# Making 31 halved products whole, moving cross attention's sums and one last addition, and one more warm product

## The chip, the cores and the metric

The kernel runs on one NeuronCore of one Trainium2 chip. The metric is the device time of one execution in microseconds (us). Kernels are compared by the median of several executions.

## The reference

Two decoder layers work on 256 positions of width 1024, all in float32. Each layer adds a mixer, a cross attention into a memory of 256 rows, and a gated MLP to the residual stream; a last RMSNorm follows.

```
for layer in range(2):
    hn = rmsnorm(h, norm_mix_g[layer])
    h = h + (sb_moba_mixer(hn, ...) if layer == 0 else fox_mixer(hn, ...))      # 16 heads of 64, q/k/v and output projections
    h = h + memory_cross_attention(rmsnorm(h, norm_xa_g[layer]),                # 4 heads of 64, 256 keys
                                   rmsnorm(mem, norm_mem_g[layer]), w_q, w_kv, w_out)
    h = h + conv_ffn(rmsnorm(h, norm_ffn_g[layer]), ...)                        # 1024 -> 2 x 2816 -> conv, silu, gate -> 1024
return rmsnorm(h, final_norm_g)

def rmsnorm(x, g):
    return x * rsqrt(mean(x * x) + 1e-6) * g
```

Layer 0 mixes with eight stick-breaking heads and eight heads with rotary softmax attention, layer 1 with sixteen forgetting heads.

## The kernel before

The residual stream lies transposed in SBUF: eight tiles `h[k]` of 128 channels by 256 positions. Every dense product is made in three pieces: weight and activation are each split into a high part (`whi`, `xh`, written by ScalarE) and a low part (`wlo`, `xl`, written by VectorE), and high times high, high times low and low times high are added up in PSUM. A projection to 128 output channels, `proj` (line 306), is therefore 24 products of 128x128 by 128x256: eight channel tiles, three pieces each, counted by `n`. Its transposed twin `proj_nat` (line 335) makes 128 positions by 256 channels, for the values, with 24 products as well. The weights come as blocks of 128x1024 by DMA (`block`, line 127), seven raw buffers and five split ones ahead.

Each product goes through `product` (line 298). For the places `n` that are listed in `halve` it issues two matmuls of 128 columns with the same weights instead of one of 256:

```
def product(ps, st, mv, halves, **kw):
    if halves:
        kw["skip_group_check"] = True
        for c in (slice(0, P), slice(P, T)):
            nc.tensor.matmul(ps[:, c], st, mv[:, c], **kw)
    else:
        nc.tensor.matmul(ps, st, mv, **kw)
```

Which products are halved is written by hand: for the mixers in the table `HALVES` (line 37; a dictionary for each layer, from a projection's name, such as `q3`, `k0`, `v2`, `o7` or `mk`, to its places), elsewhere as an argument. In the profile whole products have line 304 and halved ones line 302.

TensorE's order is the order of the code (a manual schedule); the other engines' order is made by a scheduler from the same code. A projection can be interrupted at a place `n` by a hook, which issues attention work or norm work there.

A norm's factor is made in three steps. `sums` (line 273) adds the squares over channels by small matmuls with ones; VectorE scales them (`ms`, line 281); GpSimd raises them to the power -1/2 (`rcol`, line 285). `spread` (line 289) turns that column into a row by two transposes on TensorE. The norm's gain is applied to the activations before the product, and the factor only when the product's result is read, so the products don't wait for it.

Cross attention (`cross`, line 827) makes two q projections over the first seven channel tiles, then the eighth for both; `sums` is a hook at 9 in the second. VectorE copies the results to `mq`. Then come the value projections of the memory, whose first has a hook at 8: `scores` makes the score products of four heads (line 799), which VectorE reduces to maxima (line 807), ScalarE exponentiates and VectorE normalises (`xp`, line 816). After the second value projection TensorE transposes the four heads' weights (line 822). The MLP (`ffn`, line 886) has `sums` as a hook at 6 of its second pair's first block, and `spread` at 11 of that pair's second block.

At the end `finish_last` (line 1037) makes the last norm: ScalarE sums the squares of a last part, GpSimd adds them to the rest (line 1050) and raises the mean to the power (line 1051), ScalarE and VectorE scale the rows, and two DMAs write them out. At the start `warm_up` (line 231) issues `WARM` matmuls of zeros, 128x512 in bfloat16, while the first data arrive.

Of the kernel before, what the change touches and what calls it, by code (L numbers as in the profile page):

```python
# [14 lines left out]
ALU = mybir.AluOpType  # L15
# [3 lines left out]
T = 256  # L19
# [3 lines left out]
DFF = 2816  # L23
KF = DFF // P
BLK = 1024
WARM = 9
RAW = 4
LATER = -200

# [4 lines left out]
          ((6, (), (0, 1), ()), (9, (), (), (0, 1)), (11, (0, 1), (2, 3), ()), (14, (), (), (2, 3)),  # L34
           (16, (2, 3), (4, 5), ()), (19, (), (), (4, 5)), (21, (4, 5), (6, 7), ()), (24, (), (), (6, 7)),
           (26, (6, 7), (), ())))
HALVES = ({"v1": (3,), "q3": (8,), "v2": (3, 27), "v3": (25, 29), "o3": (8,), "o7": (2,)},
          {"q0": (21,), "k0": (18, 21), "q1": (8,), "v1": (2,), "q3": (3,), "k3": (8,), "v2": (3,), "q6": (8,), "mk": (8,), "o2": (8,),
           "o7": (2,)})
EPS = 1e-6  # L40
SCALE = DH ** -0.5
MASKED = -1e30
# [38 lines left out]
def trunk(ctx: ExitStack, tc: tile.TileContext, a: dict, out: bass.AP):  # L81
    nc = tc.nc
# [23 lines left out]
    def bank(pl, tag, width=512):  # L106
        return pl.tile([P, 512], F32, tag=tag, name=tag)[:, :width]

    def accA():
        return bank(psA, "acc", T)  # L110

    def accS():
        return bank(psS, "sc", T)
# [491 lines left out]
    mem = Stats("m")  # L605
# [4 lines left out]
    def mixer(layer, st, xs):  # L610
# [47 lines left out]
        for g in range(4):  # L658
# [27 lines left out]
            if g == 0 and layer == 0:  # L686

                accs = [accS() for _ in range(4)]
                for n, (xh, xl) in enumerate(xs):
                    b, o = b0[n // 2], (n % 2) * 4 * P  # L690
                    steps = [(b.hi, xh), (b.hi, xl), (b.lo, xh)]
                    for group in ((0, 1), (2, 3)) if n < 2 else (range(4),):
                        for m, (wt, x) in enumerate(steps):
                            for i in group:
                                product(accs[i], wt[:, o + i * P:o + (i + 1) * P], x, n == 1 and m == 2 and i == 3,
                                        start=n == 0 and m == 0, stop=n == KD - 1 and m == 2)
                b = [block(w[i]) for i in (2, 3, 6)]
                nc.sync.dma_start(const[:, :T], a["const"][:, :T])
                st.rows(a["xt"])
                b.append(block(w[7]))  # L700
                st.sums()
                pv = [proj_nat(b, xs, t, accA()) for t in range(2)]
                early = proj(b[2], 0, xs, accA(), hooks={9: lambda: st.spread(bank(psO, "po"))}, halve=(11,))
                late_constants()
                v = [evac_col(ps, st, t, "v", 6) for t, ps in enumerate(pv)]
                for i in range(2):
                    q, k = (evac_row(accs[2 * i + j], st, "qk"[j], j == 0) for j in range(2))
                    launch(i, q, k, v)
                steps = rope_angles()
                next(steps)  # L710
                for i in range(12):
                    pipe.at(1 + i // 3, lambda: next(steps, None))
                continue
            elif g == 0:
                f = bank(psO, "po", T)

                def rates():
                    gates(f)
                    st.sums()

                q, more = pair(0, ({20: rates}, {15: st.spread}))
                k = more()
                q, k = evac_row(q, st, "q", True), evac_row(k, st, "k", False)
                decay = decay_rows(f, st)
            else:
                q, k = pair(0)
# [100 lines left out]
    def cross(layer, st, xs, ms, ks):  # L827

        hd = []
        bq = [block(a["xa_q"][layer, i]) for i in range(2)]  # L830
        acc = [proj(bq[i], 0, xs[:7], accS(), last=False, hooks={9: st.sums} if i else {}, halve=(11, 14) if i else (2,))
               for i in range(2)]
        for i in range(2):
            proj(bq[i], 7 * P, xs[7:], acc[i], first=False)
        for i in range(2):
            q = parts.tile([P, T], F32, tag="part", name="mq", bufs=NP)
            evac = nc.vector.tensor_scalar(q, acc[i], SCALE, None, op0=ALU.mult)
            hd += [Cross(j, q, ks[i], st) for j in range(2)]
        fence(2, None, evac)

        def scores():
            both_products(hd[:2])
            both_products(hd[2:])
            found = [x.scores() for x in hd]
            fence(1, None, found[-1])

        b = [block(a["xa_v"][layer, i]) for i in range(2)]
        v = [evac_col(proj_nat(b, ms, 0, bank(psO, "po", T), hooks={8: scores}, halve=(14, 17)), mem, 0, "mv", 2)]
        v.append(evac_col(proj_nat(b, ms, 1, accA(), halve=(2, 5)), mem, 1, "mv", 2))
        copied = [x.weigh(nc.vector.tensor_copy if i % 2 else nc.scalar.copy) for i, x in enumerate(hd)]  # L850
        fence(2, *copied[2:])

        def outp(pr):
            po = accA() if pr else bank(psO, "po", T)
            for m in range(2):
                for i in range(2):
                    c = slice((2 * pr + i) * DH, (2 * pr + i + 1) * DH)
                    nc.tensor.matmul(po[i * DH:(i + 1) * DH], v[m][:, c], hd[2 * pr + i].pt[:, m * T:(m + 1) * T],
                                     start=m == 0, stop=m == 1)
            r = act_pair("g", NG)  # L860
            split_ps(po, *r)
            return r

        outs = [outp(0), outp(1)]
        nst, nxt = Stats(one=True), Normed(h, G_FFN + 8 * layer, "x", NX, 2)
        b = [block(a["xa_o"][layer, i]) for i in range(2)]


        def part(j, ps, k, steps=(0, 1, 2), halve=None):
            s = slice(((j % 4) * 2 + k) * P, ((j % 4) * 2 + k + 1) * P)  # L870
            w, (xh, xl) = b[j // 4], outs[k]
            for n in steps:
                product(ps, (w.hi, w.lo, w.hi)[n][:, s], (xh, xh, xl)[n], n == halve, start=k == 0 and n == 0,
                        stop=k == 1 and n == 2)
            return ps

        acc = [part(j, (accA, accA, accS, accS)[j](), 0, (0, 1)) for j in range(4)]
        for j in range(4):
            part(j, acc[j], 0, (2,))
        for j in range(KD):  # L880
            if j >= 4:
                acc.append(part(j, (accA, accA, accS, accS)[j % 4](), 0))
            residual(j, part(j, acc[j], 1, halve=1 if j == 0 else None), nst, nxt)
        return nst, nxt.res

    def ffn(layer, st, xs):
# [58 lines left out]
        for f in range(KF):  # L945
            u = tmp.tile([P, 2 * T], F32, tag="wide", name="u", bufs=5) if f < RAW else None
            c = tmp.tile([P, 2 * T], F32, tag="wide", name="c", bufs=5)
            pss = []
            for i in range(2):
                if f == 0:  # L950
                    pss.append(first[i])
                    continue
                hooks = ({6: st.sums}, {11: st.spread})[i] if f == 1 else {}
                w = block(a["up"][layer, 2 * f + i], pieces=2 if f == 1 and i == 0 else 1)

                pair = layer == 1 and KF - 6 <= f < KF - 2
                if pair:
                    if i == 0:
                        full.append(bank(*((psO, "po"), (psA, "acc"), (psS, "sc"), (psS, "sc"))[f - KF + 6]))
                    acc = full[-1][:, i * T:(i + 1) * T]  # L960
                else:
                    acc = (accS, accA)[i if full else n % 7 % 2]()
                    n += 1
                pss.append(proj(w, 0, xs if f < RAW else xn, acc, first=not (pair and i), hooks=hooks,
                                skip=pair, halve=((8, 11), (13, 20))[i] if f == 1 else ()))
            if f == 0:
                held = u, c, pss
                continue
            if f == KF - 2:
                spare = pss[1]  # L970
            for args in ([(0,) + held] if f == 1 else []) + [(f, u, c, pss)]:
                with tc.high_priority(offset=LATER if f < 6 else 0):
                    glu(*args)
            if f == 1:
                renorm()
            if layer == 1 and 8 <= f < 8 + KD:
                turn_blocks(f - 8)
            if layer == 1 and f == 11 + KD:
                move_blocks()
# [13 lines left out]
    def down_rows(gs, acc, spare):  # L993
# [43 lines left out]
        def finish_last(multiply):  # L1037
# [3 lines left out]
            for i, (ps, c, e) in enumerate(parts[1]):  # L1041
# [5 lines left out]
                if i == 1:  # L1047
                    nc.vector.scalar_tensor_tensor(ms, both[:, 1:2], 1.0 / D, ms, op0=ALU.mult, op1=ALU.add)
                    nc.vector.tensor_mul(o[1][:, :T], ps, gain[1][:, :T])
            nc.gpsimd.tensor_tensor(mean, both[:, 2:3], ms, op=ALU.add)  # L1050
            nc.gpsimd.tensor_tensor(col, mean, half[:, 0:1], op=ALU.pow)
            nc.scalar.activation(o[0], o[0], AF.Copy, scale=col)
            nc.scalar.dma_start(out[P:T, 0:512], o[0])
# [115 lines left out]
```

## Time and profile before

| | |
|---|---|
| time, median of 3 runs | 654.72 us (653.89 to 655.59) |
| the profiled execution's own time | 655.62 us |
| its span, first to last instruction | 653.8 us |
| mean granted TensorE clock | 0.999 |
| TensorE busy, matmuls and weight loads | 646.0 and 632.5 us |
| VectorE, ScalarE, GpSimd busy | 532.6, 433.1 and 72.8 us |
| read from HBM | 119.90 MB |

In the rows below, PE is TensorE's matmuls, PEld its weight loads, DVE VectorE, ACT ScalarE, POOL GpSimd. A row of the timeline has the start in us from the span's start, the time in us, the engine, the line, the operation, the tiles (written <- read), the shape and the number of merged instructions, and in brackets the engine's idle time ahead of it with what ended it. Rows with xN are N instructions that follow each other, from the first's start to the last's end. A row of the stretches has the stretch, its length, and for each engine its busy time and the instructions in it. A row of the waits has the engine and what it waited for: us in total, times, longest.

### The profile page before, as it was taken

To read this page: it belongs to the slowest core of one execution; us is meant where nothing else is said; L and a number is where in the kernel's file an instruction comes from. 1 tells how busy PE (TensorE), PEld (TensorE's weight loads), DVE (VectorE), ACT (ScalarE), POOL (GpSimd) and SP (SyncE) were. 2 spreads that over 40 slices of the span, in tenths; PEclk is the share of its full clock that TensorE was granted. 3 is DMA by queue.
4 is the path that set the end of the run, shared out by engine and by line. 5 is a ranking of instruction groups with operands and counts; after the bars stand their busy time and mean duration, and the time that the engine had idled before them with its cause. 6 is when DMAs were issued, how large, how long until landed. Compare 5 with 4: busy or idle time off the path is not lost.

```text
span 653.8 us, 14673 instructions
## 1 busy us (share of the span) xinstructions
PE 646.0 (99%) x5665; PEld 632.5 (97%) x5665; DVE 532.6 (81%) x1105; ACT 433.1 (66%) x871; POOL 72.8 (11%) x85
## 2 busy tenths in 40 slices
PE   8999999999999999999999999999999999999996
PEld 7999999999999999999999999999999999999996
DVE  6779985999999999865679877868999999996442
ACT  6699764778777776644464676556878767784332
POOL 0001000406100000011114220022350000000000
PEclk9999999999999999999999999999999999999999
DMA  8976651555466666666648654425365667696601
GB/s 317 377 254 217 200 190 48 181 165 189 154 190 212 206 220 184 181 200 198 211 153 309 205 177 148 134 76 190 101 236 182 195 210 214 171 339 193 194 3 64
DMA packets 47669, 124.02 MB, mean 190 GB/s; under 512 B 13648, under 2 KB 17520, under 8 KB 47600
## 3 DMA queue, kind: packets, MB, share of 16 engines
q1 hardware_dynamic: 47168, 122.53, 57.8%
q8 instruction: 44, 0.72, 0.5%
q10 hardware_dynamic: 432, 0.56, 0.3%
q14 instruction: 25, 0.20, 0.1%
HBM read 119.90 MB, written 1.07 MB: 185 GB/s over the span
## 4 chain that ended last, share of the span: by engine, by line
PE 98%; DMA 1%; ACT 0%; POOLq 0%; issue 0%; DVE 0%; ACTq 0%; DVEq 0%; POOL 0%
PE acc L304 49%; PE sc L304 29%; PE acc L1010 3%; PE sc L1010 3%; PE po L1010 2%; PE po L451 2%; PE po L304 2%; PE sc L416 1%; PE sc L436 1%; PE acc L302 1%; DMA raw<-ab_first 1%; PE sc L799 1%; PE sc L822 1%; PE sc L400 0%; PE sc L379 0%; PE acc L278 0%
## 5 line engine op out<-in xcount | busy, mean ns | idle before, releaser
L136 DVE TENSOR_TENSOR wlo<-raw,whi 128x512 fp32r<-128x512 f32 (+2 forms) x288 | 269.8, 958 | 54.4 <-ACT whi L135 52.9
L135 ACT ACTIVATE whi<-raw 128x512 fp32r<-128x512 f32 (+2 forms) x288 | 225.5, 815 | 91.9 <-PE acc L304 37.9
L304 PE MATMUL sc<-xn,whi 128*128 128x256 f32 x656 | 112.9, 276 | 0.0
L304 PEld LDWEIGHTS sc<-xn,whi 128*128 128x128 f32 x656 | 98.9, 188 | 0.0
L304 PE MATMUL sc<-xn,wlo 128*128 128x256 f32 x328 | 90.5, 276 | 0.0
L304 PE MATMUL acc<-xn,whi 128*128 128x256 f32 x464 | 80.3, 276 | 0.0
L304 PE MATMUL acc<-xh,whi 128*128 128x256 f32 x284 | 79.8, 281 | 0.0
L304 PE MATMUL acc<-xl,whi 128*128 128x256 f32 x286 | 79.3, 277 | 0.0
L304 PE MATMUL acc<-xh,wlo 128*128 128x256 f32 x281 | 78.1, 278 | 0.0
L304 PEld LDWEIGHTS acc<-xn,whi 128*128 128x128 f32 x464 | 70.0, 188 | 0.0
L304 PE MATMUL acc<-gh,whi 128*128 128x256 f32 x240 | 67.1, 280 | 0.0
L304 PE MATMUL acc<-gl,whi 128*128 128x256 f32 x240 | 66.3, 278 | 0.0
L253 POOL TENSOR_TENSOR sq<-sq 128x256 f32<-128x256 f32 x35 | 31.4, 896 | 304.5 <-ACT sq L247 288.7
L304 PE MATMUL acc<-gh,wlo 128*128 128x256 f32 x234 | 64.6, 277 | 0.0
L304 PE MATMUL acc<-xn,wlo 128*128 128x256 f32 x232 | 64.0, 276 | 0.0
L304 PEld LDWEIGHTS sc<-xn,wlo 128*128 128x128 f32 x328 | 61.6, 188 | 0.0
L304 PEld LDWEIGHTS acc<-xl,whi 128*128 128x128 f32 x286 | 53.8, 188 | 0.0
L304 PEld LDWEIGHTS acc<-xh,whi 128*128 128x128 f32 x284 | 53.4, 188 | 0.4
L304 PEld LDWEIGHTS acc<-xh,wlo 128*128 128x128 f32 x281 | 52.8, 188 | 0.0
L304 PEld LDWEIGHTS acc<-gh,whi 128*128 128x128 f32 x240 | 45.1, 188 | 1.1 <-ACT gh L183 0.8
L304 PEld LDWEIGHTS acc<-gl,whi 128*128 128x128 f32 x240 | 44.9, 188 | 0.0
L304 PEld LDWEIGHTS acc<-gh,wlo 128*128 128x128 f32 x234 | 43.9, 188 | 0.0
(291 smaller groups left out, 1544.6 us busy)
## 6 DMA issues: line engine op xcount, KB each, us to landing
raw<-up SPq DMA_DIRECT2D x88, 512.0 KB, 4.0
raw<-fox_in SPq DMA_DIRECT2D x24, 512.0 KB, 4.3
raw<-down_rows SPq DMA_DIRECT2D x22, 512.0 KB, 4.4
raw<-ab_in SPq DMA_DIRECT2D x20, 512.0 KB, 6.6
raw<-down SPq DMA_DIRECT2D x16, 448.0 KB, 3.4
raw<-ab_out SPq DMA_DIRECT2D x8, 512.0 KB, 4.6
raw<-down SPq DMA_DIRECT2D x8, 512.0 KB, 3.5
raw<-fox_out SPq DMA_DIRECT2D x8, 512.0 KB, 4.1
```

The lines of the kernel that those rows point to most:

```text
L135: i = nc.scalar.activation(hi[:, s], raw[:, s], AF.Copy)
L136: j = nc.vector.tensor_sub(lo[:, s], raw[:, s], hi[:, s].bitcast(F32))
L253: nc.gpsimd.tensor_tensor(sq, sq, self.acc, op=ALU.add)
L302: nc.tensor.matmul(ps[:, c], st, mv[:, c], **kw)
L304: nc.tensor.matmul(ps, st, mv, **kw)
L416: nc.tensor.matmul(s[:, c], q[:, qs], k[:, 0:n], start=i == 0, stop=True, skip_group_check=True)
L436: nc.tensor.transpose(self.s[:, c:c + P], self.p[:, c:c + P], ident)
L451: nc.tensor.matmul(po[i * DH:(i + 1) * DH, j * T + q:(j + 1) * T], v[m][:, vc + i * DH:vc + (i + 1) * DH], hd.pt[:, c], start=m == 0 and j ...
L799: nc.tensor.matmul(s[:, t * T:(t + 1) * T], self.q[:, t * P:(t + 1) * P], self.k, start=t == 0, stop=True, skip_group_check=True)
L822: nc.tensor.transpose(self.s[:, m * T + t * P:m * T + (t + 1) * P], self.p[:, t * T + m * P:t * T + (m + 1) * P], ident)
L1010: nc.tensor.matmul(ps[:, o:o + T], x[:, s], y[:, c + o:c + o + T], start=False, stop=k == KF - 1 and x is gl, skip_group_check=True)
```

## The change

- 31 of the 46 halved products become whole; 15 stay halved. Five entries go from the table for layer 0 (both places of `v2`, both of `v3`, the one of `o7`) and five from that for layer 1 (`q0`, 21 of `k0`, `q3`, `k3`, `o7`). `early` loses one, each layer's cross attention all seven (three in the q projections, four in the values), and each layer's MLP three of four (20 of the second block stays).
- Cross attention's `sums` moves from place 9 of the second q projection into `scores`, in front of the score products, and that hook moves from place 8 to place 4.
- The addition of `mean` in `finish_last` moves from GpSimd to VectorE.
- `WARM` goes from 9 to 10.

```
-WARM = 9
+WARM = 10
...
-HALVES = ({"v1": (3,), "q3": (8,), "v2": (3, 27), "v3": (25, 29), "o3": (8,), "o7": (2,)},
-          {"q0": (21,), "k0": (18, 21), "q1": (8,), "v1": (2,), "q3": (3,), "k3": (8,), "v2": (3,), "q6": (8,), "mk": (8,), "o2": (8,),
-           "o7": (2,)})
+HALVES = ({"v1": (3,), "q3": (8,), "o3": (8,)},
+          {"k0": (18,), "q1": (8,), "v1": (2,), "v2": (3,), "q6": (8,), "mk": (8,), "o2": (8,)})
...
-                early = proj(b[2], 0, xs, accA(), hooks={9: lambda: st.spread(bank(psO, "po"))}, halve=(11,))
+                early = proj(b[2], 0, xs, accA(), hooks={9: lambda: st.spread(bank(psO, "po"))})
...
-        acc = [proj(bq[i], 0, xs[:7], accS(), last=False, hooks={9: st.sums} if i else {}, halve=(11, 14) if i else (2,))
-               for i in range(2)]
+        acc = [proj(bq[i], 0, xs[:7], accS(), last=False) for i in range(2)]
...
         def scores():
+            st.sums()
             both_products(hd[:2])
...
-        v = [evac_col(proj_nat(b, ms, 0, bank(psO, "po", T), hooks={8: scores}, halve=(14, 17)), mem, 0, "mv", 2)]
-        v.append(evac_col(proj_nat(b, ms, 1, accA(), halve=(2, 5)), mem, 1, "mv", 2))
+        v = [evac_col(proj_nat(b, ms, 0, bank(psO, "po", T), hooks={4: scores}), mem, 0, "mv", 2)]
+        v.append(evac_col(proj_nat(b, ms, 1, accA()), mem, 1, "mv", 2))
...
-                                skip=pair, halve=((8, 11), (13, 20))[i] if f == 1 else ()))
+                                skip=pair, halve=(20,) if f == 1 and i else ()))
...
-            nc.gpsimd.tensor_tensor(mean, both[:, 2:3], ms, op=ALU.add)
+            nc.vector.tensor_add(mean, both[:, 2:3], ms)
```

On TensorE, in layer 0's cross attention, the built order around the sums (`acc<-const,sq`) and the scores (`sc<-mk,mq`) is before:

```order
L304 MATMUL sc<-xh,wlo 128x256
L278 MATMUL acc<-const,sq 128x1 x2
L304 MATMUL sc<-xh,whi 128x256
L304 MATMUL sc<-xl,whi 128x256
L302 MATMUL sc<-xh,wlo 128x128 x2
L304 MATMUL sc<-xh,whi 128x256
L304 MATMUL sc<-xl,whi 128x256
L302 MATMUL sc<-xh,wlo 128x128 x2
```

The sums stood inside the second q projection, with two halved products close behind them. Now the place where the sums stand reads:

```order
L303 MATMUL po<-whi,gh 128x256
L303 MATMUL po<-wlo,gh 128x256
L303 MATMUL po<-whi,gl 128x256
L303 MATMUL po<-whi,gh 128x256
L277 MATMUL acc<-const,sq 128x1 x2
L798 MATMUL sc<-mk,mq 128x256 x8
L303 MATMUL po<-wlo,gh 128x256
```

The sums have moved behind the whole q projection and four value products, right in front of the scores; lines are one lower in the changed file.

On VectorE, at the same place, the order is before (`ms` is the scaled sum, `mq` the copied q, `mx` the maxima):

```order
L188 SCALAR_TENSOR_TENSOR xl<-h_97,small,xh 128x256
L136 TENSOR_TENSOR wlo<-raw,whi 128x512 x4
L281 TENSOR_SCALAR ms<-acc 128x2
L837 TENSOR_SCALAR mq<-sc 128x256 x2
L136 TENSOR_TENSOR wlo<-raw,whi 128x512 x2
L807 TENSOR_REDUCE mx<-sc 128x2 x2
L808 TENSOR_TENSOR mx<-mx,rcol 128x2 x2
```

and now:

```order
L187 SCALAR_TENSOR_TENSOR xl<-h_97,small,xh 128x256
L135 TENSOR_TENSOR wlo<-raw,whi 128x512 x4
L835 TENSOR_SCALAR mq<-sc 128x256 x2
L135 TENSOR_TENSOR wlo<-raw,whi 128x512
L280 TENSOR_SCALAR ms<-acc 128x2
L135 TENSOR_TENSOR wlo<-raw,whi 128x512
L806 TENSOR_REDUCE mx<-sc 128x2 x2
L807 TENSOR_TENSOR mx<-mx,rcol 128x2 x2
```

The scaled sum has moved behind `mq` and one weight split, and has one split between itself and the reduces.

## The prediction

> **What bounds the kernel now.** I read the page first: its busy shares and the chain that ended last.
>
> ```profile
> PE 646.0 (99%) x5665; PEld 632.5 (97%) x5665; DVE 532.6 (81%) x1105; ACT 433.1 (66%) x871; POOL 72.8 (11%) x85
> PE 98%; DMA 1%; ACT 0%; POOLq 0%; issue 0%; DVE 0%; ACTq 0%; DVEq 0%; POOL 0%
> ```
>
> 98% of the chain is TensorE itself. The view of waits, for PE, agrees: it has two entries, both at the program's start.
>
> ```profile
> PE acc L236 <- DVE warm L233: 1.2, 1, 1.2
> PE sc L304 <- ACT whi L223: 0.6, 1, 0.6
> ```
>
> So the question is what one product costs on PE. The view of stretches gives it for a long undisturbed piece of the second MLP, and the timeline of PE shows a halved product in a calm place (the value projection at 61 us).
>
> ```profile
> 500.00:640.00 140.00, 140.00 (x1237) 140.00 (x1237) 110.11 (x177) 86.70 (x134) 0.00 (x0) 1.00 0.59 185
> 61.06 0.28 PE L304 MATMUL acc<-wlo,xh 128*128 128x256 f32 x1
> 61.17 0.28 PE L304 MATMUL acc<-whi,xl 128*128 128x256 f32 x1
> 61.28 0.34 PE L302 MATMUL acc<-whi,xh 128*128 128x128 f32 x2
> 61.45 0.33 PE L304 MATMUL acc<-wlo,xh 128*128 128x256 f32 x1
> 61.62 0.28 PE L304 MATMUL acc<-whi,xl 128*128 128x256 f32 x1
> ```
>
> A whole product takes 140.00/1237 = 0.113 us from start to start. (The 0.28 us beside each is a modelled latency; products overlap.) Every matmul has its own weight load, and PEld is busy 140.00 of 140.00 us, so the loads set this step. The halved product at 61.28 and the whole one behind it take 61.62 - 61.28 = 0.34 us where two whole ones take 0.227. **A halved product costs one step more, 0.113 us**: it loads the same weights twice.
>
> Here the Trainium skill speaks against the change: TensorE: Matmul & The Clock Gate, section Back-to-back issue gap, gives a gap of N/2.4 + 2.5 ns, by which two halves (112 ns) cost 2.5 ns more than one whole (109 ns) and 31 of them 0.08 us; the row, 0.113 us each, disagrees and decides.
>
> There is a second pace. In layer 1 a projection that is halved at its 18th and 21st product (335.30, 335.76) is followed by 48 value products from 336.22 to 341.87.
>
> ```profile
> 335.30 0.34 PE L302 MATMUL acc<-xh,whi 128*128 128x128 f32 x2
> 335.76 0.33 PE L302 MATMUL acc<-xh,whi 128*128 128x128 f32 x2
> 336.22 0.28 PE L304 MATMUL sc<-whi,xh 128*128 128x256 f32 x1
> 341.87 0.29 PE L304 MATMUL acc<-xh,whi 128*128 128x256 f32 x1
> ```
>
> 5.65/48 = 0.1177 us: a **slow pace**, 0.0044 us more per product, with no wait shown. The next rows, each a first and a last of a piece, show it in three more places.
>
> ```profile
> 24.62 0.28 PE L304 MATMUL acc<-xh,whi 128*128 128x256 f32 x1
> 25.56 0.28 PE L304 MATMUL acc<-xh,wlo 128*128 128x256 f32 x1
> 133.46 0.28 PE L304 MATMUL po<-whi,gh 128*128 128x256 f32 x1
> 133.93 0.28 PE L304 MATMUL po<-wlo,gh 128*128 128x256 f32 x1
> 360.16 0.28 PE L304 MATMUL acc<-xh,whi 128*128 128x256 f32 x1
> 360.52 0.33 PE L302 MATMUL acc<-xh,whi 128*128 128x128 f32 x2
> ```
>
> 8 products in 0.94 us, 4 in 0.47, 3 in 0.36: 0.117 to 0.120 each. In these places the halving that follows comes while the pace is slow, and the normal step returns within a few products. So a halving costs 0.113 us at once, and may be paid back at 0.0044 us a product: only after 26 products.
>
> **The change, part by part.** The sum is made against the profiled execution, 655.62 us (span 653.8), which lies 0.9 us above the median of 654.72.
>
> *Products made whole.* The built order has 46 halved products before and 15 after, so 31 (not 37) change. I sort them by what is around them.
>
> (a) 22 stand in the normal pace or behind a short interruption, with nothing that waits close behind: in layer 0 four value products and one of the output projection, in layer 1 `q0`, `k3`, `o7`, in each cross attention six of seven, in each MLP the 13th product. 22 x 0.113 = 2.49 us gained. Bounds: 2.5 if the pace is as it is, and 0.35 less if four of them (behind spread or sums) would leave about 20 products each at the slow pace (4 x 20 x 0.0044).
>
> (b) Five end a slow pace or prolong one. Layer 0's `early` (11): 0.113 less some 36 products to the next interruption (0.16), a loss of 0.05. Cross attention's value product 14, twice: 0.113 less 39 x 0.0044 = 0.17, a loss of 0.06 each. Layer 1's `q3`: 0.113 - 21 x 0.0044, a gain of 0.02. Layer 1's `k0` at 21: the halving at 18 stays and has five products to return to the normal step, so 0.113 plus the 48 slow ones (0.21) less some 8 slow ones in the next projection (0.04), a gain of 0.28. Together +0.13; if the pace returns by itself everywhere +0.6, if `k0` too stays slow -0.1.
>
> (c) Four (8 and 11 in each MLP's second block) stand between the sums and the spread of the norm, and the spread waits:
>
> ```profile
> 156.15 1.62 POOL L285 TENSOR_TENSOR rcol<-ms,half 128x2 f32<-128x2 f32 x1 [3.57 <-DVE ms L281]
> 157.84 0.23 PEld L292 LDWEIGHTS acc<-const,rcol 128*128 128x128 f32 x2
> ```
>
> POOL ends at 157.77, PE loads 0.07 us later; layer 1 runs the same code. Without the halvings PE arrives 0.23 us sooner and waits for POOL: I count 0 (bounds 0 and 0.45). What is late next is POOL's power.
>
> *Cross attention's sums.* Before, they stand in the second q projection; the rows from there to the last transposes:
>
> ```profile
> 126.66 0.74 POOL L253 TENSOR_TENSOR sq<-sq 128x256 f32<-128x256 f32 x1 [0.73 <-ACT sq L247]
> 127.07 2.68 DVE L136 TENSOR_TENSOR wlo<-raw,whi 128x512 fp32r<-128x512 f32 x4 [0.35 <-ACT whi L135]
> 127.45 0.52 PEld L278 LDWEIGHTS acc<-const,sq 128*128 128x128 f32 x4
> 127.92 0.36 PE L304 MATMUL sc<-xh,whi 128*128 128x256 f32 x1
> 129.67 0.15 DVE L281 TENSOR_SCALAR ms<-acc 128x2 f32<-128x2 f32 x1
> 129.90 0.70 POOL L285 TENSOR_TENSOR rcol<-ms,half 128x2 f32<-128x2 f32 x1 [2.50 <-DVE ms L281]
> 130.16 0.77 DVE L837 TENSOR_SCALAR mq<-sc 128x256 f32<-128x256 f32 x2 [0.34 <-PE sc L304]
> 130.84 1.28 DVE L136 TENSOR_TENSOR wlo<-raw,whi 128x512 fp32r<-128x512 f32 x2
> 132.47 1.29 DVE L807 TENSOR_REDUCE mx<-sc 128x2 f32<-128x512 f32 x2 [0.34 <-PE sc L799]
> 138.83 0.62 DVE L816 TENSOR_SCALAR xp<-xp,sm 128x256 f32<-128x256 f32 x2
> 139.23 0.25 PEld L822 LDWEIGHTS sc<-const,xp 128*128 128x128 f32 x2
> ```
>
> They wait for POOL (end 127.40, load 127.45) and cost about 0.5 us with the restart behind them. Moved in front of the score products they wait for nothing and share one restart: a gain of about 0.12 each. The price is on DVE. PE ends the q products 0.86 us sooner (three halvings 0.34, sums 0.52), but DVE is in its four `wlo` until 129.75, so `mq` starts at about 129.7, not 129.3. Then `mq` 0.77, `wlo` 0.64, the moved `ms` 0.15, `wlo` 0.64: the first reduce starts at about 131.9, 0.57 us sooner than 132.47. Behind `ms` are queued that `wlo` and the reduces; POOL's power (0.70) ends before the second reduce does, so `rcol` delays nobody. The hook at 4 instead of 8 gives four products more between scores and transposes, where four halvings went: even. PE wants the transposes 0.8 us sooner, the softmax gives 0.57, and the spare there is about 0.15 (the load after the one at 139.23 against the first half of DVE's 138.83 + 0.62). So PE waits about 0.1 us more per layer (bounds 0 and 0.35). Net +0.02 each.
>
> *Last addition on VectorE.*
>
> ```profile
> 646.96 0.16 DVE L1048 SCALAR_TENSOR_TENSOR fin<-fin 128x1 f32<-128x1 f32 x1 [0.40 <-ACT sq L1019]
> 648.10 0.19 ACT L1019 ACTIVATION_READ_ACCUMULATOR sq<-acc 128x1 f32 x1
> 648.37 0.19 POOL L1050 TENSOR_TENSOR fin<-fin 128x1 f32<-128x1 f32 x1 [4.13 <-ACT sq L1019]
> 648.64 0.55 POOL L1051 TENSOR_TENSOR fin<-fin,half 128x1 f32<-128x1 f32 x1
> ```
>
> ACT ends at 648.29. DVE, idle, would start some 0.04 later, take 0.16, and hand over to POOL as in cross attention (129.82 to 129.90): 648.57 instead of 648.64, +0.07 (bounds -0.1 and +0.15).
>
> *One more warm product.*
>
> ```profile
> 1.18 4.02 PE L236 MATMUL acc<-warm 128*128 128x512 bf16 x9 [1.18 <-DVE warm L233]
> 5.84 0.79 PE L304 MATMUL sc<-xh,whi 128*128 128x256 f32 x2 [0.65 <-ACT whi L223]
> 10.27 0.54 PE L304 MATMUL sc<-xl,whi 128*128 128x256 f32 x2
> ```
>
> Nine take about 0.43 us apart; the tenth lies inside the 0.65 us that PE waits for `whi`, so it costs 0. From 5.84 to 10.27 twenty products start, 0.22 us each: TensorE has half its clock until about 10.5 us. I count no gain; a rival does.
>
> Sum: 2.49 + 0.13 + 0 + 0.04 + 0.07 = **2.7 us**. From the median: **652.0 us**. Its own range is 650.7 (gain 4.0: (b) +0.6, (c) +0.45, no wait in cross attention) to 653.2 (gain 1.5: the lower ends together).
>
> **The rivals.** *The clock rises sooner* (chance 0.15). Before, PE stands still between the ninth warm product and 5.84; filling half of that may count as unbroken work. For: the full clock came 4.7 us after that pause, though PE had worked before it. Against: half of the pause stays. At most the 22 slow products gain 0.1 us each, 2.2; I take 1.8, as ACT's and DVE's splits follow close: 650.2 us. The Trainium skill (the same page, Part 1, What's actually happening) has the gate watch free-running windows of about 3.4 us; by an estimate from it, a release one window sooner is worth 16 x 0.1 = 1.6 us, and the trace's release 9.3 us after the first matmul is later than two such windows.
>
> *Waits take the halvings' place* (0.12). In cross attention and the MLP's start DVE feeds PE closely, and 14 of the 22 in (a) stand there. If they all turn into waits, 1.58 us go: 653.6 us. Against: PE's list of waits has none there.
>
> *The slow pace is locked into an MLP* (0.04), the slower side. The spread at 157.84 interrupts PE; before, products 13 and 20 behind it are halved, after only 20. If the normal step does not return, the slow pace runs on through layer 0's MLP, some 1515 products to 330.7 us: 1515 x 0.0044 = 6.7 us, 658.7 us. It decides from about 600 slow products on (2.7/0.0044). Against: one halving is left, and single ones end the slow pace at 360.52.
>
> *Halvings are nearly free* (0.03): the second load replaces a wait that comes anyway. Then only the tail and the sums remain, 654.6 us; the row at 61.28 speaks against it.
>
> **How the numbers follow.** The forecast has 0.66. A change of 0.3% (2.0 us, to 652.8) is about what a measurement can tell. Faster: 0.66 x 0.9 + 0.15 + 0.12 x 0.2 = 0.77. Same: the rest of the forecast and of the second rival, and the free halvings, 0.19. Slower: 0.04. The range for 8 in 10 goes from 649.6, inside the clock case, to 653.5, nearly through the second rival.
>
> **What would show it.** Right: PE's half rows fall from 92 to 30; the span shrinks by steps of 0.11 us at each place of (a); the spread's load still follows POOL by 0.07 us; reduce and transposes in cross attention come 0.6 to 0.7 us sooner against the q products; PE stays at 0.113 us from 165 us to 330. Wrong: a pace of 0.118 there, PE waiting in its list for DVE or POOL by more than 1 us, or a first product at full clock before 8 us.

## The result, and the profile after

| | before | changed |
|---|---|---|
| time, median of 5 runs each | 654.72 us (653.55 to 655.59) | 650.28 us (650.01 to 651.28) |
| span of the profiled execution | 653.8 us | 649.4 us |

The ratio is 0.9938, with a 95% interval of 0.9921 to 0.9955: a gain of 4.44 us (0.6%) where 2.7 were forecast. First the changed kernel's page, its view of waits for PE, and its view of stretches for the piece that was shown of before:

```profile
PE 641.0 (99%) x5635; PEld 627.5 (97%) x5635; DVE 531.5 (82%) x1106; ACT 433.2 (67%) x871; POOL 71.2 (11%) x84
PE 96%; DMA 2%; issue 1%; ACT 0%; DVE 0%; POOLq 0%; POOL 0%; ACTq 0%; DVEq 0%
```

```profile
PE acc L235 <- DVE warm L232: 1.2, 1, 1.2
PE sc L303 <- ACT whi L222: 1.0, 2, 0.5
PE sc L798 <- DVE mq L835: 0.3, 1, 0.3
```

```profile
500.00:640.00 140.00, 140.00 (x1238) 140.00 (x1237) 106.14 (x171) 83.25 (x130) 0.55 (x1) 1.00 0.58 180
```

TensorE is still the bound, and its step in the calm piece is the same 0.113 us. Two waits are new: one for `whi` in the first projections, one for `mq` in cross attention. PE's timeline shows that the start has changed, too:

```profile
1.18 4.20 PE L235 MATMUL acc<-warm 128*128 128x512 bf16 x10 [1.18 <-DVE warm L232]
5.92 0.50 PE L303 MATMUL sc<-xh,whi 128*128 128x256 f32 x2 [0.54 <-ACT whi L222]
6.26 0.40 PE L303 MATMUL sc<-xl,whi 128*128 128x256 f32 x2
6.49 0.39 PE L303 MATMUL sc<-xh,wlo 128*128 128x256 f32 x2
```

The third product starts at 6.26 and the fifth at 6.49: 0.115 us each, where before still took 0.21 us until 10.5. The kept trace says the same in the throttle's own record, from which the granted clock of the views is taken: it begins with the full clock, at 10.58 us before and at 4.99 us in the changed kernel. Ahead of that it has no entry, and the views print 1.00 there; "full clock" below is this entry. To see where the 4.4 us of span came from, I divide both traces at the first product of each stage, in us. The last two columns are the changes in two experiments below (halvings alone, sums alone):

| stage | before | changed | forecast | measured | halvings alone | sums alone |
|---|---|---|---|---|---|---|
| start, to the first value product | 19.17 | 17.76 | 0 | -1.41 | | |
| layer 0, mixer | 104.78 | 104.09 | -0.51 | -0.69 | -0.69 | 0.00 |
| layer 0, cross attention, q | 6.35 | 5.44 | | -0.91 | -0.11 | -0.53 |
| layer 0, cross attention, rest | 17.53 | 17.99 | -0.64 with q | +0.46 | -0.18 | +0.48 |
| layer 0, MLP | 180.71 | 180.57 | -0.11 | -0.14 | -0.12 | 0.00 |
| layer 1, mixer | 114.42 | 113.77 | -0.64 | -0.65 | -0.65 | 0.00 |
| layer 1, cross attention, q | 6.41 | 5.44 | | -0.97 | -0.06 | -0.59 |
| layer 1, cross attention, rest | 17.54 | 17.65 | -0.64 with q | +0.11 | -0.15 | +0.47 |
| layer 1, MLP, to the last product | 180.59 | 180.45 | -0.11 | -0.14 | -0.11 | 0.00 |
| behind the last product's start | 6.30 | 6.24 | -0.07 | -0.06 | | |

The start is left out of the two last columns because it differs between executions of one kernel, as the experiments show. Behind it the stages add up to -2.99 us, against the forecast's -2.7. So the sum of the steps was nearly right, and the start's 1.41 is most of what it lacked in this pair of executions.

### The profile page after: what moved, and what is told of

It reads as the page before. It is cut to its first block, busy times and chain, and to the rows that moved or that the text cites. A ratio compares the mean times of both kernels' runs of the same rounds, so it can differ in the third digit from the quotient of the medians.

```text
span 649.4 us, 14609 instructions
## 1 busy us (share of the span) xinstructions
PE 641.0 (99%) x5635; PEld 627.5 (97%) x5635; DVE 531.5 (82%) x1106; ACT 433.2 (67%) x871; POOL 71.2 (11%) x84
## 4 chain that ended last, share of the span: by engine, by line
PE 96%; DMA 2%; issue 1%; ACT 0%; DVE 0%; POOLq 0%; POOL 0%; ACTq 0%; DVEq 0%
PE acc L303 49%; PE sc L303 28%; PE acc L1009 3%; PE sc L1009 3%; PE po L1009 2%; PE po L450 2%; PE po L303 2%; PE sc L415 1%; PE sc L435 1%; DMA h<-x 1%; DMA raw<-ab_first 1%; PE sc L798 1%; PE sc L821 1%; PE sc L399 0%; PE acc L301 0%
## 5 line engine op out<-in xcount | busy, mean ns | idle before, releaser
L252 POOL TENSOR_TENSOR sq<-sq 128x256 f32<-128x256 f32 x35 | 30.1, 861 | 302.1 <-ACT sq L246 286.2
```

Source lines behind the costliest of these rows:

```text
L252: nc.gpsimd.tensor_tensor(sq, sq, self.acc, op=ALU.add)
```

## The experiments

The theory after the result (A): the tenth warm product brings the full clock forward and is worth 1.4 to 1.5 us; halvings and sums make the other 2.9 about as forecast. Its rivals: the moment of the full clock is chance (B), or halvings and sums alone make all of the 4.4.

### The tenth product alone, and taken away

The kernel before, with

```
-WARM = 9
+WARM = 10
```

> The kernel before with ten warm products instead of nine and nothing else. Theory A (the tenth product decides when the full clock comes): the products run at 0.113 us from 6.2 us on and not only from 10.6, worth 2.1 us at that place, of which about 0.6 goes back into a wait for ACT's whi near 13 us as in the changed kernel; 1.5 us faster, about 653.2. Theory B (the moment of the full clock has nothing to do with the tenth product, the traces of before and after only happened to differ): within 0.4 us of 654.7, and a trace that may show either moment.

Measured: 653.67 us (653.25 to 654.16, 12 runs) against 654.12 (653.27 to 656.19, 23 runs) of before; ratio 0.999, 0.9979 to 1.000. Neither 1.5 us nor a clean nothing. The changed kernel with `WARM = 9`:

> The changed kernel with nine warm products again. Theory A: steps of 0.213 us until about 10.6 us, no wait near 13 us, 1.5 us slower than the changed kernel: 651.8, a gain of 2.9 on the kernel before. Theory B: 650.3, as with ten.

Measured: 650.89 us (649.80 to 652.08, 6 runs), 0.6 above the changed kernel's 650.28. The six lie in two groups, 649.8 to 650.0 and 651.8 to 652.1. The traces say why. PE's timeline of the first (ten products):

```profile
5.85 0.79 PE L304 MATMUL sc<-xh,whi 128*128 128x256 f32 x2 [0.22 <-ACT whi L223]
...
6.86 0.53 PE L304 MATMUL sc<-xh,wlo 128*128 128x256 f32 x2
7.23 0.39 PE L304 MATMUL sc<-xh,whi 128*128 128x256 f32 x2
```

of the second (nine), whose profiled execution belongs to the longer group:

```profile
9.33 0.63 PE L303 MATMUL sc<-xh,wlo 128*128 128x256 f32 x2
9.76 0.50 PE L303 MATMUL sc<-xh,whi 128*128 128x256 f32 x2
10.09 0.40 PE L303 MATMUL sc<-xl,whi 128*128 128x256 f32 x2
```

and of the kernel before with only the halvings gone (nine as well; its experiment comes next):

```profile
1.18 3.43 PE L235 MATMUL acc<-warm 128*128 128x512 bf16 x9 [1.18 <-DVE warm L232]
```

Where the clock is full, rows of two products come 0.23 us after each other instead of 0.43. The traces' clock records put that place at 7.16 us, at 9.96 us, and in the last trace at 3.87 us, inside the warm products (nine of them in 3.43 us instead of 4.02). The moment moves from execution to execution, so A in its simple form falls. Over the traces of the kernels here the full clock came with ten products between 4.34 and 7.16 us (eight traces), with nine either by 5.42 (three) or at 9.96 and 10.58 (two), never between. This is theory C: the clock is raised at the end of windows whose phase is chance; a pause of some 0.8 us (the ninth product, 0.43 us long, ends near 4.99, the first real one starts at 5.75 to 5.84) spoils the window that it lies in, 0.4 us does not. The Trainium skill (TensorE: Matmul & The Clock Gate, Part 1, What's actually happening) states free-running windows of 3.4 us that don't start anew with the kernel. The traces agree: in every one the stretch at full clock is a whole number of windows of 3.413 us (638.29, 641.71, 645.12 or 648.53 us, 187 to 190 of them), the eight moments with ten products lie in one stretch of less than 3.4 us, and the two late ones with nine are one window behind 6.55 and 7.17, windows in which the pause lies. How long a pause spoils a window is not shown: with the halvings alone the window from 0.46 to 3.87 us counted, although the first matmul started only at 1.18.

C was tested with six warm products in the changed kernel (`WARM = 6`).

> The changed kernel with six warm products instead of ten: TensorE stands still from 3.7 to about 5.8 us. Theory C (the clock is raised at the end of windows of some 3.4 us whose phase differs from execution to execution, and a window with a long enough pause doesn't count): the full clock comes between 7.2 and 10.7 us in every execution, median 651.4 to 652.1, none near 650.0. Theory B (the moment is chance and has nothing to do with the warm products): median near 650.3 with single executions at 651.5 to 652. Theory D (the warm products don't matter at all, only the work from 5.8 us on): the same as C, so a C that is right must also explain the full clock before 7 us with nine or ten.

Measured: 651.91 us (650.37 to 652.98, 6 runs), and in the trace full clock at 11.53 us. The median is where C put it and B did not. Two points of C's forecast were missed: 11.53 lies outside its 7.2 to 10.7, and two of the six ended at 650.4 and 650.6, where it allowed none. A window that closes at about 4 us, before the long pause fills much of it, would explain the two (3.87 and 4.34 us stand in two traces above), but no trace of such an execution of this kernel was kept, so that stays open.

Last, changed kernel and nine products side by side.

> The changed kernel itself, beside the next one. Theory C: ten warm products leave a pause of some 0.5 to 0.9 us by TensorE's starts, and in every execution the full clock comes before 7.3 us; executions between 649.8 and 651.3, median 650.3.

> The changed kernel with nine warm products. Theory C: about half of the executions get the full clock only at about 10 us and end near 651.9, the others like the changed kernel near 650; median 0.3 to 1.2 us above the changed kernel. Theory B (the tenth product decides nothing): the same spread as the changed kernel, medians within 0.3 us.

Measured: with ten 650.70 us (650.18 to 650.93, 6 runs), with nine 650.55 (650.39 to 652.21, 6 runs), one of them above 651. The medians don't differ, against C's 0.3 to 1.2; the late execution is there, but one in six, not half. Taken together, what the tenth product appears to do is to take away the late executions: of the kernel before 22 of 68 runs in these comparisons lie above 655 us, of its version with ten products none of 12 above 654.2. In the first comparison, two of before's five were such runs and one more was at 654.72, while the median of all 68 is 654.0. Against that, the changed kernel's median (650.6 over its 11 runs) is a gain of 3.4 us; 4.44 had about 1 us of luck in it.

### Halvings alone

The kernel before with the 31 halvings gone, and `sums`, `scores`, last addition and `WARM` as before.

> The kernel before with the 31 halvings gone and nothing else: sums and scores at their old places, last addition on GpSimd, nine warm products. The prediction's terms (a), (b), (c) together: 2.49 + 0.13 + 0 = 2.6 us faster, 652.1. If waits take the halvings' place in cross attention and the MLP's start: 1.0, 653.7. If halvings and sums alone made all of the 4.4 us: 650.4 or little above.

Measured: 651.90 us (12 runs), ratio 0.9967, 0.9954 to 0.998, so 2.2 us (1.3 to 3.0); by the stages of the table, 2.07. Mixers and MLPs give what the change gives. Cross attention does not: 0.29 and 0.21 us, where the halvings were forecast at 0.62 each. The timeline at the sums in layer 0 and layer 1 shows where the part of the q projections went (0.11 and 0.06 us gained there by three halvings each):

```profile
123.71 0.74 POOL L252 TENSOR_TENSOR sq<-sq 128x256 f32<-128x256 f32 x1 [0.73 <-ACT sq L246]
124.50 0.52 PEld L277 LDWEIGHTS acc<-const,sq 128*128 128x128 f32 x4 [0.26 <-POOL sq L252]
442.51 0.52 PEld L277 LDWEIGHTS acc<-const,sq 128*128 128x128 f32 x4 [0.32 <-POOL sq L252]
```

The brackets are the point. Before, the load at 127.45 followed POOL without an idle time; now it stands 0.26 and 0.32 us waiting for POOL's last square. TensorE comes sooner, because `o7` and the first q projection have lost a halving each, but the squares don't. Those halvings were padding in front of the sums. What is missing behind the q projections (0.18 and 0.15 us gained by four halvings) was not taken apart.

### Sums alone

The kernel before with the sums moved and the scores' hook at 4, all halvings kept.

```
-        acc = [proj(bq[i], 0, xs[:7], accS(), last=False, hooks={9: st.sums} if i else {}, halve=(11, 14) if i else (2,))
+        acc = [proj(bq[i], 0, xs[:7], accS(), last=False, halve=(11, 14) if i else (2,))
...
+            st.sums()
             both_products(hd[:2])
...
-        v = [evac_col(proj_nat(b, ms, 0, bank(psO, "po", T), hooks={8: scores}, halve=(14, 17)), mem, 0, "mv", 2)]
+        v = [evac_col(proj_nat(b, ms, 0, bank(psO, "po", T), hooks={4: scores}, halve=(14, 17)), mem, 0, "mv", 2)]
```

> The kernel before with cross attention's sums moved in front of the scores and the scores' hook from 8 to 4, all halvings kept, nothing else. The prediction's term: 0.04 us for both layers. Theory P (halvings in front of the sums were padding while GpSimd made the squares; with them kept the sums wait for little, so moving them gains only a restart and the wait itself): 0.2 to 0.5 us faster. Theory M (the move is worth the same with and without halvings): about 1.3 us faster, as between the kernel with the halvings alone gone and the changed kernel with nine warm products.

Measured: 655.00 us (12 runs), ratio 1.0004, 0.9995 to 1.0014: no gain. The median is blurred, probably by the start: seven of these 12 runs took 655.0 us and more, of before's 23 only six. By stages, which leave the start out, -0.05 and -0.12 us, 0.17 in all: just under P's lower end and not far from the prediction's 0.04; M falls. The starts of the first q and the first value product show the shift, in the kernel before,

```profile
123.95 0.28 PE L304 MATMUL sc<-xh,whi 128*128 128x256 f32 x1
130.30 0.28 PE L304 MATMUL po<-whi,gh 128*128 128x256 f32 x1
```

with the sums alone,

```profile
121.76 0.28 PE L304 MATMUL sc<-xh,whi 128*128 128x256 f32 x1
127.58 0.28 PE L304 MATMUL po<-whi,gh 128*128 128x256 f32 x1
```

with the halvings alone,

```profile
120.87 0.28 PE L303 MATMUL sc<-xh,whi 128*128 128x256 f32 x1
127.11 0.28 PE L303 MATMUL po<-whi,gh 128*128 128x256 f32 x1
```

and in the changed kernel:

```profile
121.84 0.28 PE L303 MATMUL sc<-xh,whi 128*128 128x256 f32 x1
127.28 0.28 PE L303 MATMUL po<-whi,gh 128*128 128x256 f32 x1
```

That is 6.35, 5.82, 6.24 and 5.44 us. The sums' 0.53 us reappear behind the scores' hook (+0.48); alone the move is nearly even, the halvings alone give 0.11 here, and both together 0.91. With the sums out of the projection, nothing in it waits any more, and the three halvings give their full 0.38. The separate gains of cross attention are 0.50 (halvings) and 0.17 (sums); together they are 1.31 in this pair of executions (the section on the wait for `mq` shows why other executions of the same code give 1.7).

### What a halving costs

The changed kernel with 72 more: `halve=(13,)` in every block of the MLPs from the third pair on, except those that share a bank.

> The changed kernel with 72 more halved products, the 13th of 72 projections in the calm parts of both MLPs. If a halved product costs one step more (0.113 us, and up to 0.126 with the three slightly slow steps that follow in a projection): 8.1 to 9.1 us slower than the changed kernel, 658.4 to 659.4. If a halving is nearly free (2.5 ns): 0.2 us, 650.5.

Measured: 659.43 us (6 runs), 9.15 above the changed kernel, 0.127 each. Layer 0's MLP holds 40 of them. Its first product and the first of the next mixer, here

```profile
144.27 0.28 PE L303 MATMUL acc<-xh,whi 128*128 128x256 f32 x1
329.86 0.28 PE L303 MATMUL acc<-xh,whi 128*128 128x256 f32 x1
```

are 185.59 us apart. In the changed kernel this stage takes 180.57 us; the difference is 5.02 us, 0.1255 for each. Nearly free halvings are refuted.

The prediction set a formula of the Trainium skill (TensorE: Matmul & The Clock Gate, Back-to-back issue gap) against its own rows. That was a misreading: the section gives N/2.4 + 2.5 ns for an isolated matmul, and says that in a stream of weight loads and matmuls both set the spacing. So it does not speak against the change. The same page of the Trainium skill, section LDWEIGHTS (loading the stationary operand), gives a load the number of its columns divided by 1.2, in ns; by an estimate from that, 128 columns take 107 ns. The measured step of 113 ns is near it, and two loads take two steps.

### What ends the slow pace

The changed kernel with layer 1's `k0` halved at 21 again.

> The changed kernel with layer 1's k0 halved at 21 again, beside the kept 18. The prediction's step: the halving costs 0.113 and turns the 48 value products behind it to the slow pace (0.1177 instead of 0.113, 0.21 us), so the stretch from the projection's 18th product to the end of those values takes 0.28 to 0.32 us longer than in the changed kernel. Rival: the values keep 0.113, 0.11 us longer.

Measured in a single run (651.13 us): layer 1's mixer takes 114.07 instead of 113.77 us, 0.30 more. The first value product and the first product behind the 48 are

```profile
333.11 0.28 PE L303 MATMUL sc<-whi,xh 128*128 128x256 f32 x1
338.76 0.28 PE L303 MATMUL acc<-xh,whi 128*128 128x256 f32 x1
```

5.65/48 = 0.1177 us, the slow pace; the changed kernel steps 0.113 here. The prediction's step holds. It also shows that a halving does not always end the slow pace: the one at 18 does, and a second one three products later brings it back.

Then the last halvings made whole. The edit empties the table `HALVES` and takes the halvings out of cross attention and the MLPs, 14 of the 15; the one in the first projections of layer 0, at 8.5 us, stays halved in this run.

> The changed kernel with its last 15 halvings made whole too. If the slow pace of 0.1177 us a product goes away by itself or at the next interruption: 15 times 0.113, less some 20 slow products at each place, about 0.5 us faster, 649.8. If only a halving ends it behind the spread (rival of the prediction: the slow pace locked into an MLP): about 1500 products of layer 0's MLP and 1400 of layer 1's at 0.0044 us more, 12.8 - 1.7 = 11 us slower, 661.

Measured: 658.46 us median, but in two groups, five runs from 651.8 to 652.9 and seven from 658.4 to 659.4. The profiled execution is of the first: no MLP locked, yet layer 1's mixer takes 114.93 us instead of 113.77, because the slow pace now runs on through whole projections: of the mixers' ten places, nine show a stretch of 45 to 154 products at 0.117 to 0.119 us each. So nearly all of the halvings that stayed in the mixers end a slow pace, and even where no MLP locks, the kernel without them is slower by more than 1 us. The second group is 6.6 us above the first. To find its place, only the halving at 20 in each MLP's start was taken away:

```
-                                skip=pair, halve=(20,) if f == 1 and i else ()))
+                                skip=pair, halve=()))
```

> The changed kernel with the last halving of each MLP's start (place 20 of its second block) whole too, the other 13 kept. If that halving is what ends the slow pace behind the spread: some executions 6.0 to 6.7 us longer (657), with 0.1177 us a product from the spread to the end of the MLP, the others 0.2 us shorter or equal (650.2). If the long executions of the kernel with all halvings gone come from the mixers or cross attention: all near 650.2.

Measured: six runs from 649.54 to 650.63 and six from 656.49 to 657.34. This time the profiled execution is a long one, and the view of stretches shows both MLPs:

```profile
200.00:260.00 60.00, 60.00 (x532) 60.00 (x531) 57.16 (x96) 42.97 (x71) 0.00 (x0) 1.00 0.65 205
500.00:560.00 60.00, 60.00 (x511) 60.00 (x511) 57.05 (x104) 41.13 (x69) 0.00 (x0) 1.00 0.60 176
```

The changed kernel for the second stretch:

```profile
500.00:560.00 60.00, 60.00 (x532) 60.00 (x531) 58.91 (x107) 43.41 (x72) 0.00 (x0) 1.00 0.63 181
```

Same clock, PE and its loads busy throughout, no wait, and 511 products instead of 532: 0.1174 us each. Layer 1's MLP takes 186.96 us instead of 180.45, from the spread to the last product. Layer 0's is at the normal step (180.39). So the slow pace can be locked into a whole MLP; with the one halving behind the spread no execution of the changed kernel was a long one (none of 11, against six of 12 without it). Whether it locks without it differs by execution, and what decides that is open.

### The wait for `mq`

The changed kernel with `hooks={7: scores}`.

> The changed kernel with the scores' hook at 7 instead of 4. In the changed kernel's trace the score products of layer 0 wait 0.33 us for mq; three more value products (0.34 us) ahead of them fill that wait. If the wait was a loss of its own: layer 0's cross attention 0.3 us shorter (17.99 to about 17.65 behind the q projections), layer 1's unchanged, 0.3 us in all. If the softmax sets the end of the stage anyway: the transposes wait as much longer, and nothing changes.

Measured: 650.51 us (649.92 to 651.17, 4 runs). The rest of cross attention takes 17.93 us in layer 0 (17.99 with the hook at 4) and 17.97 in layer 1 (17.65), where no change was forecast. The wait for `mq` is gone and has come back at the last head's transposes, whose loads now wait (the bracket names ACT, but their weights `xp` come from DVE, which has the first half of the last head at about 136.36):

```profile
136.05 0.62 DVE L815 TENSOR_SCALAR xp<-xp,sm 128x256 f32<-128x256 f32 x2
136.52 0.42 PEld L821 LDWEIGHTS sc<-const,xp 128*128 128x128 f32 x4 [0.31 <-ACT mv L360]
```

So more products ahead of the scores don't help: when `mq` comes late, the softmax sets the end of this stage. But `mq` doesn't always come late, and that is what layer 1 shows here. The same code stands in eight traces, two layers each. In ten of the 16, `mq` starts 5.84 to 5.92 us behind the first q product and the rest of cross attention takes 17.60 to 17.65 us; in six it starts 6.26 to 6.31 us behind it, the scores wait, and the rest takes 17.93 to 18.03. The profiled execution of the changed kernel has the late form in layer 0. With nine warm products, layer 0 has the early one:

```profile
122.94 0.28 PE L303 MATMUL sc<-xh,whi 128*128 128x256 f32 x1
128.79 0.74 DVE L835 TENSOR_SCALAR mq<-sc 128x256 f32<-128x256 f32 x2
129.27 2.00 PE L798 MATMUL sc<-mk,mq 64*128 64x256 f32 x16
```

With the hook at 7 both layers have the late form (6.27 and 6.30). So the late `mq` is a loss of its own, 0.3 to 0.4 us, in some executions; what makes DVE late in them is open. No version here beats the changed kernel by an amount that could be measured.

## Why the prediction was right or wrong

**The direction and the bulk of the sum were right.** Behind the start, 2.99 us against 2.7. The measured 650.28 lies outside the forecast's own range (650.7 to 653.2), on the 650.2 of the rival "the clock rises sooner", and one of the prediction's signs of being wrong is there: a first product at full clock before 8 us. Most of the surplus is the luck of the first comparison: the gain between the medians of all runs, 3.4 us, lies inside the forecast's own 1.5 to 4.0.

**The halving's cost** (0.113 us) was right in kind and 0.013 low within projections, where the slightly slow steps behind a halving add up to 0.126. The 72 halvings show it.

**The slow pace** held as a step: `k0` 0.28 forecast, 0.30 measured; layer 1's mixer 0.64 and 0.65. One place was wrong. Layer 0's `early` was to lose 0.05 because the slow pace would run on; the changed kernel leaves it by itself behind the spread's transposes:

```profile
23.20 0.28 PE L303 MATMUL acc<-xh,whi 128*128 128x256 f32 x1
...
24.14 0.28 PE L303 MATMUL acc<-xh,wlo 128*128 128x256 f32 x1
...
24.84 0.28 PE L303 MATMUL acc<-xh,whi 128*128 128x256 f32 x1
24.95 0.28 PE L303 MATMUL acc<-xl,whi 128*128 128x256 f32 x1
```

Eight products in 0.94 us ahead of the transposes, 0.1175 each; behind them 0.11 again, from the fourth product on. That is most of layer 0's 0.18 us on top of the forecast.

**The spread** came out as forecast, and only partly by the reason given. POOL ends at 155.23, and the load follows 0.06 us later:

```profile
153.62 1.61 POOL L284 TENSOR_TENSOR rcol<-ms,half 128x2 f32<-128x2 f32 x1 [3.57 <-DVE ms L280]
155.29 0.19 PEld L291 LDWEIGHTS acc<-const,rcol 128*128 128x128 f32 x2
```

But TensorE did not come 0.23 us sooner to wait for it. Without the two halvings the products between sums and spread run at the slow pace, which the prediction did not count here:

```profile
151.96 0.28 PE L303 MATMUL sc<-xl,whi 128*128 128x256 f32 x1
155.14 0.28 PE L303 MATMUL acc<-xl,whi 128*128 128x256 f32 x1
```

That is 27 products in 3.18 us, 0.1178 each, about 0.12 us more than at 0.113. The last of them starts 0.15 us ahead of the transposes, where 0.118 is a step, so only some 0.03 us is left as a wait.

**Cross attention** came out at 1.31 us against 1.28, but not by the steps given. "Six of seven" halvings at their full 0.113 each and a nearly even move of the sums were costed one after the other against the kernel before. The row of the load at 127.45, close behind POOL, was quoted for the sums; it also forbade the halvings their gain as long as the sums stayed. Alone they give 0.50 of the forecast 1.24. That the total fits is luck in one more way: in layer 0 of this execution `mq` starts at 128.10, 6.26 us behind the first q product, and the score products wait 0.33 us for it,

```profile
128.10 0.74 DVE L835 TENSOR_SCALAR mq<-sc 128x256 f32<-128x256 f32 x2
128.57 2.00 PE L798 MATMUL sc<-mk,mq 64*128 64x256 f32 x16 [0.33 <-DVE mq L835]
```

while layer 1, without this wait, gains 0.86. The prediction's 129.7 for `mq` was 5.75 us behind the first q product, close to the early form (5.84 to 5.92); that there is a late one it did not know. The sign that reduce and transposes come 0.6 to 0.7 us sooner shows the same: 0.32 and 0.46 in layer 0, 0.73 and 0.86 in layer 1. With the early form in both layers, as in the trace with nine warm products, the gain is 1.70. A wait of 0.1 us was put at the transposes instead.

**The last addition** gained as forecast: POOL's power starts 0.28 us behind ACT's end at 643.94, before 0.35.

```profile
643.75 0.19 ACT L1018 ACTIVATION_READ_ACCUMULATOR sq<-acc 128x1 f32 x1
643.98 0.16 DVE L1049 TENSOR_TENSOR fin<-fin 128x1 f32<-128x1 f32 x1 [0.86 <-ACT sq L1018]
644.22 0.56 POOL L1050 TENSOR_TENSOR fin<-fin,half 128x1 f32<-128x1 f32 x1 [4.33 <-DVE fin L1049]
```

**The step that failed** is "so it costs 0 ... I count no gain" for the warm product. What it forecast of the start was read from one execution, as if the full clock at 10.5 us belonged to the kernel; it belonged to that execution. The rival "the clock rises sooner" is what the profiled pair shows: 22 products gain 2.1 us (the rival's "at most 2.2"), and 0.7 of it is lost again, 0.43 in a new wait for `whi`, whose maker ACT had been held up by the residual's load:

```profile
12.08 0.91 ACT L186 ACTIVATE xh<-h,small 128x256 fp32r<-128x256 f32 x2 [1.29 <-DMA h<-x]
...
13.56 0.39 PE L303 MATMUL sc<-xh,whi 128*128 128x256 f32 x1 [0.43 <-ACT whi L222]
```

But its worth over many executions is far smaller, from nothing to about 0.6 us by the three comparisons above, since most executions of the kernel before (46 of 68 below 655 us) don't show the late clock's time.

**The rivals.** Waits do take the halvings' place, in cross attention's q projections and only without the move of the sums. The slow pace locked into an MLP is real, at 6.5 us; the prediction put it in layer 0 and gave it 0.04 because one halving was left. With that halving no long execution was seen.

## What to carry to other kernels

Work that looks like pure waste may stand in front of a wait or end a slow state; before it is taken out, look which row behind it follows another engine closely, and cost edits that share a wait together, not one by one. Where the first microseconds hold a clock that rises at a moment of chance, or a wait comes in some executions only, one trace is one draw: compare stage by stage behind the start, and read the start from several executions.

## What the runs showed of the hardware

- A stream of these products has two stable steps, 0.113 and 0.1174 to 0.1177 us, at the same granted clock of 1.00 and without any wait. Sums or a spread's transposes can switch between them. A halved product mostly ends the slow one within a few products, but one that came three products behind another brought it back (0.1177 us over 48 products). Without a halving behind the spread the slow one lasted through all of layer 1's MLP, 6.5 us.
- The full clock came between 3.9 and 11.5 us after the span's start, at moments that differ between executions of one kernel, and lasted whole multiples of 3.413 us (187 to 190). With nine warm products it slipped to 10 us in two of five traces, with ten in none of eight, with six to 11.5 in the one trace kept.
